# First loads on a second DMA queue, and the first tile stored in three pieces (contrast adjustment, one core)

## Chip, cores and metric

One NeuronCore of a Trainium2 chip. The metric is the device time of one execution in microseconds (us); lower is better. The kernel runs on one core, so there is one span and one clock.

## What is computed

```python
x: 16 x 3 x 512 x 512 float32, factor = 1.5
mean = np.mean(x, axis=(2, 3), keepdims=True)
out = np.clip(mean + factor * (x - mean), 0, 1).astype(np.float32)
```

Each of the 48 images of 512 x 512 is scaled about its own mean and clipped. Every pixel has to be read before the first pixel of its image can be written: 50.33 MB in, 50.33 MB out.

## The kernel before

The 48 images are cut into 6 tiles of 128 rows of 16384 numbers (64 KB a row, 8 MB a tile); 16 rows make an image, so a tile holds 8 whole images. `ring` holds three tiles (`BUFS`), tile t in place t % 3. Tiles 0 to 2 are loaded, computed and stored, then tiles 3 to 5 in the same places; the clip works in place, and the store reads the place itself.

For a tile (`compute`, line 92):

- `add` (line 82) sums each row: VectorE (DVE) the first 4352 columns with a `tensor_reduce` (L85), ScalarE (ACT) the other 12032 with a Copy `activation` that accumulates (L89). Tile 0 is summed in two halves of 8192 columns.
- The matmuls of L100 (PE) add the row sums of an image across its 16 partitions, with the weight (1 - factor)/262144 in `blockw`, into one number for each partition, `bias`.
- VectorE computes `factor * x + bias` (L103), then max with 0 and min with 1 (L106), and the result is stored (`store`, line 79, DMAs on L80).

The loop over `cuts` repeats clip and store for pieces of the columns: `compute(0, SHORT)` has a first piece of 2048 columns (8 KB a row) and a second of 14336 (56 KB).

The order is written by hand (`manual_schedule`): every engine executes its own instructions in the order of the program text, and waits where it needs another's result. All DMAs, loads (L77) and stores (L80), are issued by SyncE (SP) on one queue, in this order:

```python
load(0, 0, SHORT); load(0, SHORT, HALF); load(0, HALF, ROW); load(1); load(2)
store of tile 0 (two pieces); store of tile 1; store of tile 2
load(3); load(4); load(5)
store of tile 3; store of tile 4; store of tile 5
```

A store waits on SyncE for its clip. Load 3 needs the place of tile 0, so store 0 must have landed; load 4 waits for store 1, load 5 for store 2.

Of the kernel before, what the change touches and what calls it, by code (L numbers as in the profile page):

```python
# [1 line left out]

# [4 lines left out]


P = 128  # L10
ROW = 16384
HALF = ROW // 2
BUFS = 3
SHORT = 2048
SUM = 4352


@with_exitstack
def kernel(
    ctx: ExitStack,  # L20
    tc: tile.TileContext,
    x: bass.AP,
    factor: float,
    out: bass.AP,
):

    nc = tc.nc
    f32 = mybir.dt.float32  # L30
    Alu = mybir.AluOpType
    Act = mybir.ActivationFunctionType

    B, C, H, W = x.shape
    n_img, n_pix = B * C, H * W
    ppi = n_pix // ROW
    per_tile = P // ppi
    n_tiles = n_img // per_tile
    assert ppi * ROW == n_pix and per_tile * n_tiles == n_img

    factor = float(factor)
    wconst = (1.0 - factor) / float(n_pix)

    x_f = x.rearrange("b c h w -> (b c h w)")
    out_f = out.rearrange("b c h w -> (b c h w)")

    def dram(ap, t, c0=0, c1=ROW):
        return bass.AP(tensor=ap.tensor, offset=t * P * ROW + c0, ap=[[ROW, P], [1, c1 - c0]])

    consts = ctx.enter_context(tc.tile_pool(name="consts", bufs=1))  # L50
    xpool = ctx.enter_context(tc.tile_pool(name="xpool", bufs=1))
    small = ctx.enter_context(tc.tile_pool(name="small", bufs=1))
    psum = ctx.enter_context(tc.tile_pool(name="psum", bufs=1, space=bass.MemoryType.PSUM))


    sums = small.tile([P, 4 * n_tiles], f32, name="sums")
    bias = psum.tile([P, n_tiles], f32, name="bias")

    blockw = consts.tile([P, P], f32, name="blockw")
    blocks = blockw.rearrange("p (a b) -> p a b", b=ppi)  # L60
    nc.gpsimd.memset(blockw, wconst)  # L61
    for base, step in ((0, -ppi), (ppi - 1, ppi)):
        nc.gpsimd.affine_select(  # L63
            out=blocks,
            in_=blocks,
            compare_op=Alu.is_ge,
            fill=0.0,
            base=base,
            pattern=[[step, per_tile], [0, ppi]],
            channel_multiplier=1 if step < 0 else -1,  # L70
        )


    ring = xpool.tile([P, BUFS, ROW], f32, name="ring")

    def load(t, c0=0, c1=ROW):
        nc.sync.dma_start(out=ring[:, t % BUFS, c0:c1], in_=dram(x_f, t, c0, c1))  # L77

    def store(t, c0=0, c1=ROW):
        nc.sync.dma_start(out=dram(out_f, t, c0, c1), in_=ring[:, t % BUFS, c0:c1])  # L80

    def add(t, col, c0, c1, c2):
        xt = ring[:, t % BUFS, :]
        own = sums[:, 4 * t + col : 4 * t + col + 2]
        nc.vector.tensor_reduce(  # L85
            out=own[:, 0:1], in_=xt[:, c0:c1], axis=mybir.AxisListType.X, op=Alu.add
        )
        part = xt[:, c1:c2]
        nc.scalar.activation(out=part, in_=part, func=Act.Copy, accum_out=own[:, 1:2])  # L89
        return [own[:, 1:2], own[:, 0:1]]  # L90

    def compute(t, *cuts):
        xt = ring[:, t % BUFS, :]
        if t == 0:
            parts = add(t, 0, 0, SUM, HALF) + add(t, 2, HALF, HALF + SUM, ROW)
        else:
            parts = add(t, 0, 0, SUM, ROW)
        shift = bias[:, t : t + 1]
        for k, part in enumerate(parts):
            nc.tensor.matmul(shift, blockw, part, start=k == 0, stop=k == len(parts) - 1)  # L100
        for c0, c1 in zip((0, *cuts), (*cuts, ROW)):
            part = xt[:, c0:c1]
            nc.vector.tensor_scalar(  # L103
                out=part, in0=part, scalar1=factor, scalar2=shift, op0=Alu.mult, op1=Alu.add
            )
            nc.vector.tensor_scalar(  # L106
                out=part, in0=part, scalar1=0.0, scalar2=1.0, op0=Alu.max, op1=Alu.min
            )
            store(t, c0, c1)

    with tc.manual_schedule():
        load(0, 0, SHORT)
        load(0, SHORT, HALF)
        load(0, HALF, ROW)
        load(1)
        load(2)
        compute(0, SHORT)
        compute(1)
        compute(2)
        load(3)  # L120
        load(4)
        load(5)
        compute(3)
        compute(4)
        compute(5)


# [1 line left out]
_INS = ['x', 'factor']  # L129
_OUTS = [((16, 3, 512, 512), 'float32')]  # L130

_NUMBERS = {'factor': 1.5}


# [26 lines left out]
```

## Time and profile before

| | |
|---|---|
| time, median of 3 runs (lowest to highest) | 239.69 us (239.28 to 239.69) |
| span of the profiled execution | 237.3 us |
| median less that span | 2.4 us |
| bytes moved, mean rate over the span | 100.66 MB, 424 GB/s |
| busy: DVE, ACT, PE | 137.4, 59.9, 7.9 us |
| share of the DMA engines' time in packets | 98.7% |

The span runs from the first to the last instruction of one execution under the profiler; the times are of whole executions and hold what lies around it. The profiled execution is known by its span alone. "L89" is line 89 of the kernel. In the timeline, a line has its start, its length, the engine, the line and the operation, and in brackets the idle time before it with what ended it. SPq is SyncE's instruction queue: its lines are the issuing of DMAs, merged where they follow one another, and not the transfers. A ScalarE line L89 with idle time that a DMA ended starts when the load has landed. Each transfer is spread over the core's 16 DMA engines, eight rows on each; the packet records, one per row and engine, are the finest view of the trace.

### The profile page before, as it was taken

What the parts mean: (1) busy time and instruction counts of PE and PEld (TensorE: products, weight loads), DVE (VectorE), ACT (ScalarE), POOL (GpSimd) and SP (SyncE); (2) the same over time, 40 slices, a digit from 0 to 9 for tenths busy, and PEclk for the clock granted to TensorE, in tenths of its full rate; (3) what the DMA queues carried; (4) which work ended last, traced back from release to release, by engine and by line L of the source; (5) the groups of instructions that cost most, each with busy time, mean ns of one, the idle gap of its engine ahead of it and who ended that gap; (6) DMA issues with size and microseconds to landing.
All of it is one profiled execution on the core that took longest, in us unless ns stands there. A gap on an engine that the chain in (4) does not pass through costs nothing.

```text
span 237.3 us, 186 instructions
## 1 busy us (share of the span) xinstructions
PE 7.9 (3%) x28; PEld 6.9 (3%) x28; DVE 137.4 (58%) x21; ACT 59.9 (25%) x15; POOL 1.1 (0%) x7
## 2 busy tenths in 40 slices
PE   0010100010001000000000000100000000000000
PEld 0010100010001000000000000100000000000000
DVE  0071899949998998000000043499989998991000
ACT  2051300980492000000000049319509800000000
POOL 1000000000000000000000000000000000000000
DMA  7999989899799798989899998989899998989894
GB/s 289 418 442 442 530 353 530 353 486 398 331 464 454 341 530 353 530 353 519 365 442 442 398 486 353 530 354 530 353 475 409 431 453 376 508 353 530 353 530 177
DMA packets 2160, 100.66 MB, mean 424 GB/s; under 512 B 240, under 2 KB 240, under 8 KB 240
## 3 DMA queue, kind: packets, MB, share of 16 engines
q1 hardware_dynamic: 2160, 100.66, 98.7%
HBM read 50.33 MB, written 50.33 MB: 424 GB/s over the span
## 4 chain that ended last, share of the span: by engine, by line
DVE 43%; DMA 36%; ACT 9%; PE 2%; SPq 1%; issue 0%; DVEq 0%; ACTq 0%
DMA ring<-in_x_dram 36%; DVE ring L103 18%; DVE ring L106 18%; ACT ring L89 9%; DVE sums L85 6%; PE bias L100 2%; SPq L77 1%; SPq L80 0%; DVEq L103 0%; ACTq L89 0%
## 5 line engine op out<-in xcount | busy, mean ns | idle before, releaser
L89 ACT ACTIVATE ring<-ring 128x12032 f32<-128x12032 f32 (+1 forms) x7 | 58.0, 8280 | 128.2 <-DMA ring<-in_x_dram 128.2
L85 DVE TENSOR_REDUCE sums<-ring 128x1 f32<-128x4352 f32 x7 | 32.8, 4683 | 63.9 <-DMA ring<-in_x_dram 63.9
L103 DVE TENSOR_SCALAR ring<-ring,bias 128x16384 f32<-128x16384 f32 (+2 forms) x7 | 52.8, 7538 | 12.9 <-PE bias L100 12.9
L106 DVE TENSOR_SCALAR ring<-ring 128x16384 f32<-128x16384 f32 (+2 forms) x7 | 52.3, 7476 | 0.2
L100 PE MATMUL bias<-sums,blockw 128*128 128x1 f32 x28 | 7.9, 360 | 189.1 <-ACT ring L89 175.4
L100 PEld LDWEIGHTS bias<-sums,blockw 128*128 128x128 f32 x28 | 6.9, 314 | 190.0 <-ACT ring L89 159.4
L89 ACT ACT_TABLE_LOAD x1 | 1.3, 1283 | 0.8 <-PEq L142 0.8
L89 ACT ACTIVATION_READ_ACCUMULATOR ring<-ring 128x1 f32 x7 | 1.3, 187 | 0.0
L63 POOL TENSOR_SCALAR_AFFINE_SELECT blockw<-blockw 128x128 f32<-128x128 f32 x2 | 0.7, 340 | 0.1
L61 POOL MEMSET blockw<- 128x128 f32 x1 | 0.2, 204 | 0.3 <-POOLq L142 0.3
L142 POOL MEMSET const-bfloat16-1.0<- 128x1 bf16 x1 | 0.1, 102 | 0.0
L142 POOL MEMSET const-uint8-127<- 128x1 uint8 x1 | 0.1, 102 | 0.0
L142 POOL MEMSET const-float32-0.0<- 128x1 f32 x1 | 0.1, 98 | 0.3 <-issue 0.3
L142 POOL MEMSET const-float32-1.0<- 128x1 f32 x1 | 0.1, 98 | 0.0
## 6 DMA issues: line engine op xcount, KB each, us to landing
out_dram<-ring SPq DMA_DIRECT2D x1, 7168.0 KB, 35.9
ring<-in_x_dram SPq DMA_DIRECT2D x1, 4096.0 KB, 20.8
ring<-in_x_dram SPq DMA_DIRECT2D x1, 3072.0 KB, 11.6
ring<-in_x_dram SPq DMA_DIRECT2D x1, 1024.0 KB, 4.7
out_dram<-ring SPq DMA_DIRECT2D x1, 1024.0 KB, 34.3
ring<-in_x_dram SPq DMA_DIRECT2D x5, 57.7
out_dram<-ring SPq DMA_DIRECT2D x5, 27.0
```

Source lines behind the costliest of these rows:

```text
L61: nc.gpsimd.memset(blockw, wconst)
L63: nc.gpsimd.affine_select(out=blocks, in_=blocks, compare_op=Alu.is_ge, fill=0.0, base=base, pattern=[[step, per_tile], [0, ppi]], channel ...
L77: nc.sync.dma_start(out=ring[:, t % BUFS, c0:c1], in_=dram(x_f, t, c0, c1))
L85: nc.vector.tensor_reduce(out=own[:, 0:1], in_=xt[:, c0:c1], axis=mybir.AxisListType.X, op=Alu.add)
L89: nc.scalar.activation(out=part, in_=part, func=Act.Copy, accum_out=own[:, 1:2])
L100: nc.tensor.matmul(shift, blockw, part, start=k == 0, stop=k == len(parts) - 1)
L103: nc.vector.tensor_scalar(out=part, in0=part, scalar1=factor, scalar2=shift, op0=Alu.mult, op1=Alu.add)
L106: nc.vector.tensor_scalar(out=part, in0=part, scalar1=0.0, scalar2=1.0, op0=Alu.max, op1=Alu.min)
L142: nc = _bacc.Bacc("TRN2", target_bir_lowering=False, num_devices=1)
```

## The change

The first six transfers, all loads of tiles 0 to 2, are issued by ScalarE on its own queue; the loads of tiles 3 to 5 and all stores stay with SyncE. Tile 2 is loaded in two transfers of half a row each (32 KB). Tile 0 is clipped and stored in three pieces of 1024, 3072 and 12288 columns (4, 12 and 48 KB a row) instead of two. The sums, the matmuls and the other tiles are the same. On ScalarE the six issues come ahead of its table load and its first activation; on VectorE tile 0 has two more TENSOR_SCALAR instructions. In the changed kernel the lines below the new constant lie one to three lines lower.

```diff
 SHORT = 2048
+FIRST = (1024, 4096)
 SUM = 4352
...
     def load(t, c0=0, c1=ROW):
-        nc.sync.dma_start(out=ring[:, t % BUFS, c0:c1], in_=dram(x_f, t, c0, c1))
+        queue = nc.scalar if t < BUFS else nc.sync
+        queue.dma_start(out=ring[:, t % BUFS, c0:c1], in_=dram(x_f, t, c0, c1))
...
         load(1)
-        load(2)
-        compute(0, SHORT)
+        load(2, 0, HALF)
+        load(2, HALF, ROW)
+        compute(0, *FIRST)
         compute(1)
```

## The prediction

> **What bounds the kernel now.** I read the page's shares and queue lines first, then stretches of the span, then the order of time around the first three tiles, then the waits of SyncE's queue.
>
> ```profile
> span 237.3 us, 186 instructions
> PE 7.9 (3%) x28; PEld 6.9 (3%) x28; DVE 137.4 (58%) x21; ACT 59.9 (25%) x15; POOL 1.1 (0%) x7
> ...
> DMA packets 2160, 100.66 MB, mean 424 GB/s; under 512 B 240, under 2 KB 240, under 8 KB 240
> ...
> q1 hardware_dynamic: 2160, 100.66, 98.7%
> ```
>
> Reader: the transfers fill 98.7% of the span, on one queue; the other engines matter only where they leave that queue empty. The 1.3% is 3.1 us, at the two ends: the first row moves at 1.82 us in the packet records, the last one ends at 236.1. The middle is full, as stretches of the span show (the last two columns are the DMA share and GB/s; a packet is counted where it ends, so shares can pass 1):
>
> ```profile
> 62.40:99.80 37.40, 1.18 (x4) 1.01 (x4) 30.56 (x4) 10.32 (x2) 0.00 (x0) 1.00 1.01 439
> 99.80:140.00 40.20, 0.00 (x0) 0.00 (x0) 0.21 (x1) 0.07 (x1) 0.00 (x0) 1.00 1.02 443
> 140.00:179.00 39.00, 2.19 (x8) 1.93 (x8) 31.27 (x5) 21.01 (x5) 0.00 (x0) 1.00 1.00 430
> ```
>
> In order of time, the first three tiles and the pace of a tile:
>
> ```profile
> 27.94 1.29 DVE L103 TENSOR_SCALAR ring<-ring,bias 128x2048 f32<-128x2048 f32 x1 [0.68 <-PE bias L100]
> 30.52 63.63 SPq L80 DMA_DIRECT2D out_dram<-ring  x4
> 41.93 10.23 ACT L89 ACTIVATE ring<-ring 128x12032 f32<-128x12032 f32 x1 [15.86 <-DMA ring<-in_x_dram]
> 62.40 10.23 ACT L89 ACTIVATE ring<-ring 128x12032 f32<-128x12032 f32 x1 [10.15 <-DMA ring<-in_x_dram]
> 76.26 8.76 DVE L103 TENSOR_SCALAR ring<-ring,bias 128x16384 f32<-128x16384 f32 x1 [0.75 <-PE bias L100]
> 94.24 26.90 SPq L77 DMA_DIRECT2D ring<-in_x_dram  x3
> 139.93 10.23 ACT L89 ACTIVATE ring<-ring 128x12032 f32<-128x12032 f32 x1 [67.20 <-DMA ring<-in_x_dram]
> 159.21 10.23 ACT L89 ACTIVATE ring<-ring 128x12032 f32<-128x12032 f32 x1 [8.96 <-DMA ring<-in_x_dram]
> 168.97 46.01 SPq L80 DMA_DIRECT2D out_dram<-ring  x3
> 178.57 10.23 ACT L89 ACTIVATE ring<-ring 128x12032 f32<-128x12032 f32 x1 [9.04 <-DMA ring<-in_x_dram]
> ```
>
> A tile lands every 19.3 us (139.93, 159.21, 178.57). Each of 16 DMA engines carries 8 rows of it, so a 64 KB row takes 2.42 us. The packet records give stores the same 2.42, so direction does not set the pace. Tile 2 alone came 20.5 us after tile 1: in the packet records the last load row of each engine, just ahead of the very first store, took about 1.1 us too long.
>
> The one deadline that matters: in the packet records store 1 is through at 100.4 us (mean of the engines), and store 2 must be in the queue by then, with load 3 right behind it. Store 2 is issued at 93.8, and a first row moves about 1.1 us after an issue (first load: 0.80 to 1.82-1.95), so it is there at 94.9. Slack: 100.4 - 94.9 = 5.5 us.
>
> **The change part by part.**
>
> *Issues.* Five loads leave SyncE, six go to ScalarE. SyncE's five took 2.50 us, so ScalarE's six take about 3.0: its table load (1.28) moves from 0.8-2.1 to about 3.8-5.1, while its first data come at 12.86. Hidden with 7.8 us to spare; without that cover it would cost 3.0. The first load stays first in its queue; bounds are 0 and 1.3 later (the table load's length, if ScalarE got to it first), and below nothing no row suggests anything. The instruction order puts the loads ahead, so I take 0. On SyncE nothing waits behind the new stores but stores 1, 2 and load 3, which need them or later work anyway.
>
> *DVE.* One more piece is two more TENSOR_SCALAR. From 1.292 and 7.685 us (2048 and 14336 columns) a column costs 0.52 ns and an instruction 0.25 us beside; from 1.227 and 7.627, 0.19. So 0.44 us more on tile 0. DVE then has its reduction of tile 1 done at 50.8 instead of 50.35, and the clip of tile 1 waits for ScalarE until 53.4: hidden. The first piece is ready at 27.94 + 0.77 + 0.71 = 29.4 (before: 30.5), the second at 33.0, the third at 46.1.
>
> *Transfers.* Bytes are the same, so the total queue time is the same; what changes is whose rows go first. Before, stores of tile 0 stood behind loads 1 and 2. Now they stand in a second queue and can pass them. No row of this trace shows two queues at once, so the order has to be bounded. One end: the stores wait for whole loads, and load 2 lands at about the old 62.4. Other end: stores go first, all 19.3 us of them, and it lands at 81.7. I take one row of each queue in turn, because the records come one per row and engine: 15 transfers x 8 rows x 16 engines is 1920, the 2160 less the 240 small ones.
>
> By turns: store 0's first row moves at 29.4 + 1.1 = 30.5. Load 1 started its rows at 21.95 (mean of the engines), so four of its eight are still to go, and 16 of load 2 (two halves of eight rows of 32 KB). Twenty load rows let twenty store rows pass: eight of 4 KB at 0.151, eight of 12 KB at 0.453, four of 48 KB at 1.813, together 1.2 + 3.6 + 7.3 = 12.1 us. Load 1 gets 0.6 of it and lands at 42.5; load 2 lands at 62.4 + 12.1 = 74.5. Had load 2 stayed whole, only four turns of 4 KB and four of 12 KB would have passed its rows: the halves and the 48 KB piece are what make it late.
>
> *What is late next.* From tile 3: ScalarE starts at 139.93, the store is issued at 168.97, 29.04 later (sum, matmuls, two passes of the clip). Tile 2 is now bound by ScalarE and not by DVE, which is free at 71.5. Store 2 is issued at 74.5 + 29.0 = 103.5, first row at 104.6, while the queue, with the same bytes behind it, runs dry at 100.4. All 16 engines stand still for 4.2 us. Load 3 is behind store 2 on SyncE, so nothing else fills the hole. Store 1 makes no hole: tile 1 is clipped at about 71.5, while store 0 lasts until 81. Behind the hole everything moves by 4.2: load 4 waits for store 1, long landed, load 5 for store 2, with about 38 us of queue ahead; tile 3 was clipped at 168.9, 9.6 us before load 5 landed, and both ends move together. The last store ends 4.2 later.
>
> *Extra of the mixing.* Going from load to store cost about 1.1 us at the first store (20.47 - 19.36) and about 0.1 at load 5 into store 3. I keep the 1.1 once, as before, and charge 0 for the other turns, by the second row, where stores were no longer new; bounds are -1.1 and +2 (twenty turns at 0.1).
>
> Sum: span 237.3 + 4.2 = 241.5. The profiled execution is known by its span; the median of the runs, 239.69, lies 2.4 above it, and I carry that over: 243.9.
>
> A rule against the change: the Trainium skill, page "DMA: Bandwidth & Descriptors", section "Issuing engines are not separate DMA queues", says that transfers issued from several engines interleave on the same 16 DMA engines and only the issue time is saved. By it the two queues are worth at most the 2.5 us of issues, which the row above shows hidden: a sum of 0, without the hole.
>
> **The rivals.**
>
> *Whole transfers take turns.* Eight rows per engine go through in one go before the other queue is served. Then the 4 KB and 12 KB pieces pass ahead of load 2's end, 4.8 us, and it lands at 67.2; store 2 is issued at 96.3, there at 97.4, before 100.4. No hole: 239.7, or 238.6 if the long rows at the first store vanish. This is also how the change could do nothing. For it: nothing in the trace excludes it. Against it: rows are recorded one by one. Chance 0.20, of which 0.12 with the gain. The same page, section "Queues, rings and completion order", says that an engine drains a whole packet, typically 9 to 17 descriptors, from one ring before it switches; eight rows would fit in one, so it speaks for this rival, and no trace here shows it yet.
>
> *Equal bytes, or stores first.* While both queues hold work each moves at half pace. Store 0's last piece then shares all of load 2: load 1 lands at 46.7, load 2 at about 84, and the hole is 84 + 30.1 - 100.4 = 13.7: 253.4. Stores strictly first: 81.7, a hole of 11.4. Chance 0.10.
>
> *Costly turns.* Each of the twenty turns costs up to the 1.1 of the first switch: up to 22 us on top, 266. Chance 0.07.
>
> *Loads and stores overlap in an engine* (the other side: faster). Mixed, the engine moves more than either alone. If it hides x us of the 12.1, the end moves by 4.2 - x; from x = 4.2 on the change is no loss, and it stops at -5.5, where DVE's old chain (store 2 there at 94.9) holds: 234.2. For it: loads write what stores read. Against it: 2.42 us in both directions and no pair of packets on an engine overlapping by more than 4 ns, though one queue could hardly show it. Chance 0.13.
>
> **How the numbers follow.** Row by row: 0.50, 243.9, with its own range 239.5 to 248: two rows of 48 KB more or fewer ahead of load 2 (3.6 us either way), and the extras. Faster by over 0.2% (0.5 us, about what a measurement of this kernel can tell from no change): overlap 0.13 and whole transfers with the gain 0.12, so 0.25. Within: 0.08. Slower: 0.50 + 0.10 + 0.07 = 0.67. The range runs from 238.3, below whole transfers with the gain, to 253, near equal bytes; the overlap and the costly turns, 0.20, lie outside.
>
> **What would show it.** Right: ScalarE's sum of tile 1 starts near 42.5, of tile 2 near 74.5; store 2 is issued near 103.5; a slice of low DMA share near 100 to 105; tile 3 near 144 instead of 139.9. Wrong: tile 2 lands before 70 with no hole (whole transfers), after 80 (equal bytes), five tiles through well before 100 us (overlap) or well after it (costly turns).

## The result, and the profile after

The changed kernel takes 244.69 us (median of 4 runs, 244.60 to 244.87) against 239.52 for the kernel before (4 runs, 239.28 to 239.69): slower by a factor of 1.0215, interval 1.0200 to 1.0229. The range held it, the direction and the mechanism were as forecast, and the size fell 0.8 us short of the time (243.9) and 1.5 us short of the span (241.5, measured 243.0). Each profile is of one execution; of the changed kernel it is the one of 244.73 us.

The page of the changed kernel, the lines on span and queues:

```profile
span 243.0 us, 193 instructions
...
DMA packets 2448, 100.66 MB, mean 414 GB/s; under 512 B 272, under 2 KB 272, under 8 KB 400
...
q1 hardware_dynamic: 1584, 75.50, 72.5%
q10 hardware_dynamic: 864, 25.17, 24.5%
```

There are two queues now: q10 is ScalarE's with the three first tiles, q1 SyncE's with the rest. Together they are busy 97.0% where one was busy 98.7%. Of the bytes none was saved or added. The stretches of its span show where the missing share lies (last two columns: DMA share and GB/s):

```profile
42.30:73.70 31.40, 1.01 (x4) 0.93 (x4) 27.72 (x5) 10.32 (x2) 0.00 (x0) 1.00 1.03 440
73.70:100.40 26.70, 1.02 (x4) 0.93 (x4) 17.26 (x3) 10.32 (x2) 0.00 (x0) 1.00 0.94 406
100.40:104.10 3.70, 0.00 (x0) 0.00 (x0) 2.83 (x1) 0.00 (x0) 0.00 (x0) 1.00 0.00 0
104.10:144.00 39.90, 0.00 (x0) 0.00 (x0) 0.00 (x0) 0.00 (x0) 0.00 (x0) 1.00 1.05 445
```

The third line is the hole: 3.7 us with not a byte moved. VectorE's 2.83 in it is the end of the clip of tile 2, for which store 2 waits. The first line is the stretch in which loads and stores are mixed: 440 GB/s, no more than the 430 to 443 of the unmixed stretches before. In order of time, the lines that answer to those shown of before (ScalarE's sums of the tiles, and SyncE's issues; the second fence is the same view with a window around the hole, where store 2 stands by itself):

```profile
0.80 3.00 ACTq L79 DMA_DIRECT2D ring<-in_x_dram  x6
29.38 74.25 SPq L82 DMA_DIRECT2D out_dram<-ring  x5
42.76 10.23 ACT L91 ACTIVATE ring<-ring 128x12032 f32<-128x12032 f32 x1 [16.76 <-DMA ring<-in_x_dram]
74.25 10.23 ACT L91 ACTIVATE ring<-ring 128x12032 f32<-128x12032 f32 x1 [21.17 <-DMA ring<-in_x_dram]
85.74 8.76 DVE L105 TENSOR_SCALAR ring<-ring,bias 128x16384 f32<-128x16384 f32 x1 [9.41 <-PE bias L102]
144.51 10.23 ACT L91 ACTIVATE ring<-ring 128x12032 f32<-128x12032 f32 x1 [59.94 <-DMA ring<-in_x_dram]
163.84 10.23 ACT L91 ACTIVATE ring<-ring 128x12032 f32<-128x12032 f32 x1 [9.01 <-DMA ring<-in_x_dram]
184.06 10.23 ACT L91 ACTIVATE ring<-ring 128x12032 f32<-128x12032 f32 x1 [9.90 <-DMA ring<-in_x_dram]
```

```profile
103.30 0.33 SPq L82 DMA_DIRECT2D out_dram<-ring  x1
103.80 21.61 SPq L79 DMA_DIRECT2D ring<-in_x_dram  x3
```

Tile 1 lands 0.8 us later than before, tile 2 11.9 us later (74.25 against 62.40), store 2 is issued at 103.30 instead of 93.82. The clip of tile 2 waited 9.41 us for the bias, where before it waited 0.75: the bound of that tile passed from VectorE to ScalarE. In the packet records store 1 ends at 100.1 us (mean of the engines) and store 2's first row starts at 104.2.

The packet records also show the order row by row. The first store row moves at 34.1 us, 4.7 after its issue: the row of load 1 that was under way and one more went first. From there on each engine carries one row of each queue in turn, and the packet of 4 bytes that closes a transfer takes a turn like a row. Load 2's last row ends at 71.7 us, a row of 48 KB goes next, and only then, at 73.5, load 2's closing packet; ScalarE starts at 74.25. Until then eight store rows of 4 KB, eight of 12 KB and four of 48 KB have passed.

From there on two more delays add up. Tile 3 is summed 4.6 us later than before (144.51 against 139.93), tile 5 5.5 us later: between tiles 4 and 5 lie 20.2 us instead of 19.4. In the packet records these are long rows at the two changes of direction behind the hole: the last row of store 2 (0.73 us too long, the first row of load 3 another 0.12) and the last row of load 5 before store 3 (0.91). The sum by the packet records: rows beyond their usual length 3.46 us for each engine, against 2.05 before, +1.4; hole 4.1; together 5.5.

### The profile page after: what moved, and what is told of

It is laid out like the page before. It is cut to its first block, busy times and chain, and to the rows that moved or that the text cites. A ratio compares the mean times of both kernels' runs of the same rounds, so it can differ in the third digit from the quotient of the medians.

```text
span 243.0 us, 193 instructions
## 1 busy us (share of the span) xinstructions
PE 7.7 (3%) x28; PEld 6.8 (3%) x28; DVE 137.7 (57%) x23; ACT 59.9 (25%) x15; POOL 1.1 (0%) x7
## 4 chain that ended last, share of the span: by engine, by line
DMA 33%; DVE 33%; ACT 12%; another core or an unknown queue 9%; issue 2%; PE 1%; ACTq 1%; SPq 0%; DVEq 0%
DMA ring<-in_x_dram 33%; DVE ring L105 14%; DVE ring L108 14%; ACT ring L91 12%; DVE sums L87 4%; PE bias L102 1%; ACTq L79 1%; SPq L82 0%; DVEq L105 0%; ACTq L91 0%; SPq L79 0%
## 5 line engine op out<-in xcount | busy, mean ns | idle before, releaser
L105 DVE TENSOR_SCALAR ring<-ring,bias 128x16384 f32<-128x16384 f32 (+3 forms) x8 | 53.0, 6624 | 22.1 <-PE bias L102 22.1
L108 DVE TENSOR_SCALAR ring<-ring 128x16384 f32<-128x16384 f32 (+3 forms) x8 | 52.5, 6560 | 0.3
```

What stands on the lines that cost most here:

```text
L105: nc.vector.tensor_scalar(out=part, in0=part, scalar1=factor, scalar2=shift, op0=Alu.mult, op1=Alu.add)
L108: nc.vector.tensor_scalar(out=part, in0=part, scalar1=0.0, scalar2=1.0, op0=Alu.max, op1=Alu.min)
```

## The experiments

Theory: the engines take one row of each queue in turn, so the bytes that pass ahead of load 2's last row set when tile 2 lands, and with it the hole. Rivals: each turn between the queues costs time of its own; whole transfers take turns; the pieces themselves cost time. Times are set against the kernel before in runs on the same chip.

**Load 2 whole.**

```diff
-        load(2, 0, HALF)
-        load(2, HALF, ROW)
+        load(2)
```

> As the changed kernel, but tile 2 is loaded whole (rows of 64 KB). Row by row: only 12 rows of stores pass ahead of load 2's last row (eight of 4 KB, four of 12 KB, 3.0 us), so ScalarE starts tile 2 near 65.4 instead of 74.25, store 2 is issued near 94.5 and there is no hole near 100: span 237.0 to 238.7, time 239.2 to 241, level with the kernel before. If each turn between the queues cost time of its own (changed kernel: 5.2 us for 20 turns), 12 turns would leave some 3 us: 242.7.

Measured 239.01 us, ratio 0.9973 (0.9962 to 0.9984): a little faster than the kernel before. From its timeline:

```profile
65.28 10.23 ACT L91 ACTIVATE ring<-ring 128x12032 f32<-128x12032 f32 x1 [12.15 <-DMA ring<-in_x_dram]
95.14 25.80 SPq L79 DMA_DIRECT2D ring<-in_x_dram  x3
```

Tile 2 is summed at 65.28 (expected 65.4), load 3 is issued at 95.14, long before the queue ends. Two queues with 12 turns cost nothing. What the halves do is to give the stores eight more turns, four of them of 48 KB.

**Tile 0 in 8 and 56 KB.**

```diff
-        compute(0, *FIRST)
+        compute(0, SHORT)
```

> As the changed kernel, but tile 0 leaves in the old two pieces of 8 and 56 KB a row. Row by row: all of store 0 (8 x 0.30 + 8 x 2.12 = 19.3 us) passes ahead of load 2's end, ScalarE starts tile 2 near 81.7, store 2's first row moves 30.0 later at 111.7 while the queue runs dry at 100.1: a hole of 11.5 us, span 248.8 to 250.3, time 250.5 to 252.5. If turns cost (16 to 20 of them, as in the changed kernel): 244 to 245. If whole transfers took turns: no worse than the changed kernel.

Measured 262.81 us, ratio 1.0957 (1.0922 to 1.0993), 10 us beyond what was expected. One line of its timeline, one of its stretches:

```profile
91.27 10.23 ACT L91 ACTIVATE ring<-ring 128x12032 f32<-128x12032 f32 x1 [37.07 <-DMA ring<-in_x_dram]
```

```profile
102.60:121.10 18.50, 0.05 (x1) 0.00 (x0) 17.45 (x2) 0.00 (x0) 0.00 (x0) 1.00 0.00 0
```

The expectation stopped at the end of store 0. But tile 1 had landed, store 1 was issued at about 73, and its rows went on taking turns with load 2's last ones. Twenty turns are eight of 8 KB, eight of 56 KB and four of 64 KB: 2.4 + 16.9 + 9.7 = 29.0 us, and 62.4 + 29.0 = 91.4. Measured 91.27. In the packet records three or four rows of 64 KB pass, each on about half of the engines, and the tile has landed when the slower half is through. The hole, 20.0 us in the packet records, holds the whole of VectorE's clip of tile 2 (17.45 us in the stretch shown). Stores that pass make the load late that the next store needs.

**All on one queue, pieces and halves kept.**

```diff
-        queue = nc.scalar if t < BUFS else nc.sync
+        queue = nc.sync
```

> As the changed kernel, with its three pieces and the halves of load 2, but every transfer on SyncE's queue. Row by row needs two queues, so nothing passes: load 2 lands near 62.4, no hole, 237.3 span, 239.5. If the pieces or the halves cost time by themselves: towards 244.7. Also: the long row (about 1.1 us) that stood at the end of load 2 before the first store stays there (rows starting near 58 to 60) if it belongs to the first load-to-store switch or to its time in the run, and moves to the end of the first half (rows near 50) if it belongs to the fifth transfer of a queue.

Measured 239.70 us, ratio 0.9999 (0.9988 to 1.0009). Pieces and halves cost nothing by themselves. From its timeline:

```profile
62.55 10.23 ACT L91 ACTIVATE ring<-ring 128x12032 f32<-128x12032 f32 x1 [10.33 <-DMA ring<-in_x_dram]
```

The long row is not tied to the fifth transfer of a queue: in the packet records it is spread over the last two rows of load 2 (0.57 and 0.66 us, starting at 58.1 and 59.8), just ahead of the first store.

**Load 3 issued ahead of store 2.**

```diff
         compute(1)
-        compute(2)
         load(3)
+        compute(2)
```

> As the changed kernel, but load 3 is issued by SyncE ahead of store 2, which it does not need. Row by row: load 2 still lands near 74.2 and store 2 is still issued near 103.3, but load 3 stands in the queue from about 82 on and fills the 4.1 us: no hole, tile 3 lands near 120 instead of 144, and the span is 237.0 to 239, time 239.2 to 241.3. If turns between the queues cost the time: 244.7 as the changed kernel.

Measured 239.84 us, ratio 1.0019 (1.0002 to 1.0035). From its timeline:

```profile
74.40 10.23 ACT L91 ACTIVATE ring<-ring 128x12032 f32<-128x12032 f32 x1 [20.92 <-DMA ring<-in_x_dram]
120.58 10.23 ACT L91 ACTIVATE ring<-ring 128x12032 f32<-128x12032 f32 x1 [35.85 <-DMA ring<-in_x_dram]
```

```profile
81.58 0.34 SPq L79 DMA_DIRECT2D ring<-in_x_dram  x1
103.44 0.34 SPq L82 DMA_DIRECT2D out_dram<-ring  x1
```

Tile 2 is as late as in the changed kernel and store 2 is issued as late, and nearly all of the loss is gone, since load 3 (issued at 81.58) fills the queue meanwhile. The same 20 turns are there. So the lateness costs only by the hole, and the hole only because load 3 stood behind store 2.

**Tile 0 in four pieces.**

```diff
-FIRST = (1024, 4096)
+FIRST = (1024, 4096, 8192)
```

> As the changed kernel, with tile 0 in four pieces of 4, 12, 16 and 32 KB a row. Row by row: again 20 rows of stores pass, but the last four are 16 KB (0.6 us) instead of 48 KB (1.8), so load 2 lands 4.8 us earlier: ScalarE starts tile 2 near 69.4 instead of 74.25, store 2's first row moves near 99.4, just ahead of the 100.1 at which the queue runs dry. No hole: span 237.2 to 238.5, time 239 to 240.3. If the turns between the queues cost the time (20 again): 244.7.

Measured 241.32 us, ratio 1.0068 (1.0055 to 1.0081): between the two answers. From its timeline:

```profile
69.48 10.23 ACT L91 ACTIVATE ring<-ring 128x12032 f32<-128x12032 f32 x1 [16.37 <-DMA ring<-in_x_dram]
99.02 22.10 SPq L79 DMA_DIRECT2D ring<-in_x_dram  x3
141.26 10.23 ACT L91 ACTIVATE ring<-ring 128x12032 f32<-128x12032 f32 x1 [61.46 <-DMA ring<-in_x_dram]
```

The order of rows is right again (69.48, expected 69.4), and the packet records show no hole: store 1 ends and store 2 starts at 100.2 (means of the engines). Store 2 was issued at 98.52; with the 0.9 us from issue to first row that the changed kernel shows (103.30 to 104.2), it stood in the queue at about 99.4, only 0.8 us ahead. Yet tile 3 is summed 1.3 us later than before. The long rows are there without a hole: store 2's last (0.53), load 3's first (0.30), load 5's last (0.69).

**The queues alone: load 2 whole, 8 and 56 KB.** Both edits of the first two experiments together.

> The queues alone: loads 0 to 2 on ScalarE's queue, load 2 whole and tile 0 in the old 8 and 56 KB. Row by row: 12 rows of stores pass as in the run with load 2 whole, but four of them are 56 KB: 2.4 + 8.5 = 10.9 us, ScalarE starts tile 2 near 73.3 (one row more or less: 71.2 to 75.4), store 2's first row moves near 103.3 and the hole is 3.2 us. Span 240.5, or 241.9 if the two long rows that followed the hole in the changed kernel come with every hole; time 242.3 to 243.7. If turns and not bytes counted: 239, as with load 2 whole.

Measured 243.61 us, ratio 1.0165 (1.0150 to 1.0180). From its timeline:

```profile
72.99 10.23 ACT L91 ACTIVATE ring<-ring 128x12032 f32<-128x12032 f32 x1 [19.22 <-DMA ring<-in_x_dram]
102.47 21.67 SPq L79 DMA_DIRECT2D ring<-in_x_dram  x3
```

Twelve turns, as with load 2 whole and small pieces, but 4.6 us slower: the bytes decide, not the turns. In the packet records the hole is 2.7 us, and the long rows behind it are 0.71, 0.15 and 0.98.

**A hole in the kernel before.** One queue, no other change than work that holds the clip of tile 2 back; `c1` is 4352 and then 14336.

```diff
             parts = add(t, 0, 0, SUM, ROW)
+        if t == 2:
+            for col, c1 in ((2, SUM), (3, ROW - SHORT)):
+                part = xt[:, c1:ROW]
+                extra = sums[:, 4 * t + col : 4 * t + col + 1]
+                nc.scalar.activation(out=part, in_=part, func=Act.Copy, accum_out=extra)
```

> The kernel before, one queue, with two more ScalarE activations on tile 2 (12032 and 2048 columns, results unused) that hold its clip back. The clip starts near 85.5 instead of 76.26, store 2's first row moves near 103.9, the queue runs dry at 100.4: a hole of 3.5 us with nothing else changed. If a hole costs itself alone: span 240.8, time 243.1. If it also brings the long last rows at the two changes of direction after it (0.73 and 0.91 us more in the changed kernel): 242.2, time 244.5. If those belong to the second queue: 240.8, with no long row at the end of store 2.

Measured 244.27 us, ratio 1.0193 (1.0180 to 1.0206). A stretch and lines of its timeline:

```profile
100.80:103.70 2.90, 0.00 (x0) 0.00 (x0) 2.04 (x1) 0.00 (x0) 0.00 (x0) 1.00 0.00 0
```

```profile
103.33 21.66 SPq L77 DMA_DIRECT2D ring<-in_x_dram  x3
144.11 10.23 ACT L89 ACTIVATE ring<-ring 128x12032 f32<-128x12032 f32 x1 [58.78 <-issue]
163.41 10.23 ACT L89 ACTIVATE ring<-ring 128x12032 f32<-128x12032 f32 x1 [8.98 <-DMA ring<-in_x_dram]
183.83 10.23 ACT L89 ACTIVATE ring<-ring 128x12032 f32<-128x12032 f32 x1 [10.10 <-DMA ring<-in_x_dram]
```

The whole pattern of the changed kernel, made with one queue: an empty stretch (3.2 us in the packet records), tile 3 at 144.1, and 20.4 us from tile 4 to tile 5. The packet records show the same long rows, store 2's last 0.74 and load 5's last 1.05. They belong to the late store 2, not to the second queue.

**Load 2 whole and load 3 ahead.**

> The changed kernel with load 2 whole and load 3 issued ahead of store 2. With load 2 whole there was no hole (239.01), so nothing is left for load 3 to fill: 239.0, at most 0.3 lower if the order load 3, store 2 saves a long row, and as with load 3 ahead alone (239.84) if that order costs time by itself. Below the 239.6 of the kernel before in the first two cases.

Measured 239.63 us, ratio 1.0006 (0.9990 to 1.0022). Moving load 3 adds nothing where there is no hole and takes the small gain of load 2 whole away, which is nearest the third case; its runs also scatter more (239.19 to 241.64).

**How short a lead is too short.** The kernel before with one extra activation on the last columns of tile 2, of 8192 and of 10240 columns.

```diff
             parts = add(t, 0, 0, SUM, ROW)
+        if t == 2:
+            part = xt[:, ROW - 8192:ROW]    # or ROW - 10240
+            extra = sums[:, 4 * t + 2 : 4 * t + 3]
+            nc.scalar.activation(out=part, in_=part, func=Act.Copy, accum_out=extra)
```

> The kernel before with one more ScalarE activation on tile 2 (8192 columns, about 7.2 us, result unused): store 2 is issued near 97.7 instead of 93.8, its first row could move near 98.6, 1.8 us before the queue runs dry at 100.4. No hole. If only a hole brings long rows at the two changes of direction after it: as the kernel before, span 237.3 to 238. If they come as soon as store 2 reaches the queue with less than a row (2.4 us) left in it, as in the run with four pieces: 0.5 to 2 us more, 238 to 239.8.

> The same with 10240 columns (about 8.9 us): store 2 is issued near 99.4, first row near 100.3, level with the end of the queue, so a hole of 0 to 0.3 us. If only a hole brings the long rows and in proportion to it: 237.5 to 238.2. If they come with the short lead, whole: 239 to 239.8, that is 1.5 us over the kernel before with hardly a hole.

Measured 239.55 us, ratio 1.0010 (0.9998 to 1.0021), and 241.91 us, ratio 1.0105 (1.0076 to 1.0135). Tiles 3 to 5 of the second, from its timeline:

```profile
99.78 21.84 SPq L77 DMA_DIRECT2D ring<-in_x_dram  x3
142.03 10.23 ACT L89 ACTIVATE ring<-ring 128x12032 f32<-128x12032 f32 x1 [60.27 <-DMA ring<-in_x_dram]
161.32 10.23 ACT L89 ACTIVATE ring<-ring 128x12032 f32<-128x12032 f32 x1 [8.96 <-DMA ring<-in_x_dram]
181.72 10.23 ACT L89 ACTIVATE ring<-ring 128x12032 f32<-128x12032 f32 x1 [10.08 <-DMA ring<-in_x_dram]
```

Store 2 is issued about 0.4 us ahead of load 3, and its first row follows an issue by the same 0.9 us. So with 10240 columns it stands in the queue at about 100.3, when store 1 ends at 100.6: no hole, yet tile 3 comes 2.1 us late and tile 5 another 1.0. The packet records show the long rows (0.70, 0.34, 0.82). With 8192 columns load 3 is issued at 98.27, store 2 stands there some 2.0 us ahead, and neither row is long (0.06 at load 5's end). Over all kernels here load 5's last row is 0.06 to 0.40 us too long where store 2 came in good time, and 0.69 to 1.13 where it came late or with a short lead. The deadline for store 2 is thus not the end of the queue but somewhere between 0.8 us (four pieces) and 2.0 us before it.

The row-by-row count (62.4 us, the start in the kernel before, and the store work) beside ScalarE's measured start on tile 2:

| kernel | store work ahead of load 2 | counted | measured | hole | time |
|---|---|---|---|---|---|
| one queue | 0 us | 62.4 | 62.55 | none | 239.70 |
| load 2 whole | 3.0 | 65.4 | 65.28 | none | 239.01 |
| four pieces | 7.3 | 69.7 | 69.48 | none, late by the lead | 241.32 |
| whole, 8 and 56 KB | 10.9 | 73.3 | 72.99 | 2.7 | 243.61 |
| the change | 12.1 | 74.5 | 74.25 | 4.1 | 244.69 |
| 8 and 56 KB | 29.0 | 91.4, counted after the run | 91.27 | 20.0 | 262.81 |

## Why the prediction was right, and where it was short

- *The order of rows.* One row of each queue in turn: tile 1 at 42.76 (42.5), tile 2 at 74.25 (74.5), and the table holds it over five kernels with two queues and rows from 4 to 64 KB (one of them counted after its run). Whole transfers in turn are refuted: the change would then have had no hole, and the packet records show single rows alternating. The Trainium skill, page "DMA: Bandwidth & Descriptors", section "Queues, rings and completion order", lets an engine drain a packet of typically 9 to 17 descriptors before it turns to another ring; here it turned after a single row, of 64 KB as of 4 KB. The count of twenty store rows was right in part by luck: it took twenty load rows from 30.5 us on, but from 34.1 us on there were only nineteen, and the closing packets, which it left out, made up the rest (three of the loads, two of the stores).
- *The hole.* Forecast 4.2 us, measured 4.1, at the place named and for the reason named: load 3 ahead takes it away with tile 2 as late as in the changed kernel.
- *Equal bytes, or stores first.* Refuted by tile 2 at 74.25 instead of 84 or 81.7. By its own terms equal bytes should have given about 87 us: with tile 1 at 46.7, store 1 would have joined at about 77. The expectation for 8 and 56 KB left store 1 out in the same way.
- *Overlap of loads and stores.* Refuted: five tiles were through at 100.1 us, as before (100.4), and the mixed stretch ran at 440 GB/s. The rule of the Trainium skill, page "DMA: Bandwidth & Descriptors", section "Issuing engines are not separate DMA queues", that only issue time is saved agrees with the trace on the rate; the sum of 0 that the prediction drew from it left out the order of rows, which is where the 5 us come from.
- *ScalarE's issues, VectorE's extra instructions.* Six issues took 3.00 us and stayed hidden (first data at 12.79, before 12.86); one queue with all pieces took 239.70, so they cost nothing. The prediction's own rows give 0.39 us for VectorE's two extra instructions, not 0.44; measured 0.38.
- *The step that was short* is the term for the extras of mixing, charged with 0 beyond the old 1.1 us long row. Its bounds (-1.1 and +2) held, but it looked in the wrong place: the mixed stretch itself came out 0.3 us ahead, and the loss lay behind the hole, in the long rows of store 2 and load 5. It measured +1.4 in all. Shown: a late store 2 brings them with one queue too (244.27), and a lead of 0.3 to 0.8 us does as well, so the deadline that the prediction took (the end of store 1) was too kind.
- *From span to time.* The 2.4 us added to the span were too many: in the runs listed with their spans a time lies 1.7 to 1.8 above its own span (244.73 and 243.0; 239.49 and 237.7). By that the profiled execution of before (237.3) was a quick one: the 25 runs of that kernel beside the first experiments have spans of 237.4 to 238.8. This 0.6 hid part of what the extras lacked.

Open: why a row at a change of direction grows longer, some 17 us after store 2 came late; only the condition was shown. And why load 2 whole is 0.6 us faster than the kernel before: its profiled execution (span 237.6) was no quicker than before's (237.3), so the trace can't tell. It is the one version here that beats both kernels.

## What to carry to other kernels

Where one set of DMA engines is full, a second queue added no rate here (440 GB/s mixed, 430 to 443 before); it only lets some rows pass others, one for one, so the sizes of rows on the two queues set who is delayed. Count the bytes that pass ahead of the load whose tile is stored next, to its closing packet and not only to its last row, follow that tile to its issue, and compare it with the end of the queue less some 2 us. If a transfer that needs nothing stands behind a late one in program order, issue it first.

## What the runs showed of the hardware

Two queues share an engine row by row, with rows of 4 to 64 KB: 4 KB rows took 0.16 us and 32 KB rows 1.21 while they alternated, as long as with one queue alone. The 4-byte packet that closes a transfer waits for its turn too: 1.8 us behind a 48 KB row for load 2 of the change (71.7 to 73.5). And a queue that runs nearly dry costs more than the gap: with no gap or nearly none it cost 1.6 us (241.32 against 239.69) and 2.5 us (241.91 against 239.42), through single rows of some 0.3 to 0.8 us beyond the usual at the next two changes of direction.
